# Expert stage of a decoder layer: gate2 multiplied into w2 on GpSimd instead of into the expert output on VectorE

## The chip, the cores and the metric

The kernel runs on one core of a Trainium2 chip, as one program for all five engines of the core: TensorE (PE in the profile; its weight loads are PEld), VectorE (DVE), ScalarE (ACT), GpSimd (POOL) and SyncE (SP, which here only starts transfers). The metric is the device time of one execution in microseconds (us).

## The reference, cut to what matters

```
h2  = modulate(rmsnorm(x, norm2_w), shift2, scale2)      # 4096 tokens x 1024
# each token goes to 2 of 32 experts, with one gate each:
hid = silu(xs @ w1[e]) * (xs @ w3[e])                    # 1024 -> 512
ys  = (hid @ w2[e]) * gate[token, e]                     # 512 -> 1024
ffn = segment_sum(ys over the two experts of a token)
x   = x + gate2 * ffn                                    # gate2: one row of 1024
out = rmsnorm(x, final_norm_w)
```

gate2 is one number for each of the 1024 columns, the same for every token and every expert. So gate2 * (hid @ w2) can be had by multiplying the columns of w2 instead of the columns of the product.

## The kernel before, in words

Stages A, B and C (projections, retention, delta rule, output projection, routing) come first and the change leaves them as they are. Stage D, the experts, is the subject: `phase_d` (L1150) and what it calls.

**Order of the experts.** The experts are sorted by how many tokens they have. Each rank has a fixed number of slots (`CAPS`: 832, 512, 512, 480, 480, 448, 384, 352, three times 320, three times 288, eleven times 240, seven times 128). They are taken alternately from both ends of that list: the largest, the smallest, the second largest, and so on. An expert is cut into chunks of at most three tiles of up to 128 rows (a tile is what the second layer adds at a time). So there are 16 pairs: seven of a large expert and one of 128 slots, seven of an expert with three tiles (352 to 288) and one of 240 (two tiles), and two of 240 and 240.

**Weights.** `load_expert` (L1327) brings an expert in 12 blocks of 128 x 1024 numbers: eight for w1 and w3, then four for w2. For each block SP starts a transfer into one of five `rawD` buffers (L1333), ScalarE makes the rounded half `whD` (L71, in the helper `split`), and VectorE makes the rest `wlD` = rawD - whD (L72). Both halves go to slots of a pool of 27, of which one expert takes 24 and the three gather buffers `xg` the others, so a block of the next expert can only be split when TensorE has used up a block of the present one. The first eight blocks of the next expert are asked for while the last chunk of the present one runs, the four of w2 at the start of the expert's own first chunk (`load(r, 12)`, L1228).

**One chunk.** `d_hidden` (first layer): for each of four column groups 24 matmuls into `ph` for w1 and 24 for w3, Silu on ScalarE, the product `hs` on VectorE (L1448), then `hh` and `hl`, its two halves. Chunks of 128 slots go another way with rows and columns exchanged (L1471 to L1479). `d_rows` (second layer): for each tile two halves of 512 columns, each 12 matmuls into one of two `py` buffers (L1535 to L1537). Then `add` (L1539): VectorE takes `py` times the token's gate times gate2 into `yg` (L1542), and adds `yg` to `ag` (L1543), the 128 rows of the running sum. Between the tiles TensorE transposes the next chunk's rows (`ptx`, L1413), which ScalarE and VectorE split into `xh` and `xl`.

**The running sum** lies in device memory (`acc_d`). Its rows are gathered by GpSimd into one of four `ag` buffers (`d_acc`, L1490), and scattered back when the tile is added (`keep`, L1570). Columns beyond 1024 hold a flag from which `d_to` (L1503 to L1506) computes where to write. In the next chunk VectorE scales the finished rows in place (L1380) and GpSimd scatters them to the output (L1381). All GpSimd work of the stage is one queue: gathers of `xg` (L1397) and of `ag`, the flags, `keep`, the output.

**What sets the order.** The instructions of each engine are put in a fixed order by a scheduler when the program is built; `pin` (L1350) ties a GpSimd instruction behind the one that the program wrote before it on GpSimd. On the chip each engine takes its instructions in that order.

Of the kernel before, what the change touches and what calls it, by code (L numbers as in the profile page):

```python
# [9 lines left out]
F32 = mybir.dt.float32  # L10
# [4 lines left out]
ALU = mybir.AluOpType  # L15
# [4 lines left out]
P = 128  # L20
D = 1024
# [32 lines left out]
class Kern:  # L54
# [1097 lines left out]
    def phase_d(self):  # L1152
        tc, nc, T = self.tc, self.nc, self.T
        caps = [min(c, T) for c in self.CAPS]
        with tc.tile_pool(name="D", bufs=2) as p:
# [15 lines left out]
            n = 0  # L1171
            for r in order:
                col0[r] = n
                rows = [min(P, caps[r] - P * b) for b in range(nt[r])]
                i = 0
# [13 lines left out]
            def load_slots(i):  # L1189

                r = order[i]
                c = slice(col0[r], col0[r] + nt[r])
                reg[r] = nc.values_load(self.eid[0:1, r:r + 1], engines=[mybir.EngineType.SP], min_val=0, max_val=NE - 1)
                nc.sync.dma_start(slots[:, c], tab[bass.ds(reg[r], 1), :, 0:nt[r]].rearrange("o l b c -> (o l) b c"))
                nc.vector.tensor_copy(ids[:, c], slots[:, c, 0])
# [3 lines left out]
            def load(r, k):  # L1199

                if r not in ld:
                    ex[r] = {"w1": {}, "w3": {}, "w2": {}}
                    ld[r] = self.load_expert(p, reg[r], ex[r])
                for _ in range(k):
                    next(ld[r], None)
# [15 lines left out]
            for i, s in enumerate(st):  # L1221
                nx = st[i + 1] if i + 1 < len(st) else None
                r = s["r"]
                if s["first"]:
                    k = order.index(r)
                    if k + 2 < len(order):
                        load_slots(k + 2)
                    load(r, 12)  # L1228
                if i == 2:
                    li, limb, col = self.overflow(p, caps)  # L1230
                if nx:
                    self.d_gather(p, nx, ids)

                jobs = []
                if s["last"] and nx:
                    jobs += [lambda: load(nx["r"], 2)] * 4

                pv = st[i - 1] if i else None
                acc = [lambda t=t, m=m: self.d_acc(p, s, t, m, ids) for t, m in s["tiles"]]
                free = self.AGS - (len(pv["tiles"]) if pv else 0)  # L1240
                ends = [acc[:free], acc[free:] + [lambda: self.d_to(p, s, slots)]]
                if pv:
                    ends[0].insert(0, lambda: self.d_norm(p, pv))
                    ends[1].insert(0, lambda: self.d_root(p, pv))
                    ends[1][1:1] = [lambda q=q: self.d_out(p, pv, q) for q in range(len(pv["tiles"]))]
                self.d_hidden(p, s, ex[r], jobs[:2], ends)
                turn = self.d_turn(p, nx) if nx else []
                self.d_rows(p, s, ex[r], slots, turn, jobs[2:], nx is None)
            self.outs = None
            n = nc.values_load(li[0:1, 2 * P:], min_val=0, max_val=P - 1)  # L1250
            with tc.For_i(0, n, 1) as i:
# [10 lines left out]
                s = dict(tiles=[(0, P)], n=P, rows=False)  # L1262
# [64 lines left out]
    def load_expert(self, p, e, w):  # L1327


        nc = self.nc  # L1330

        def block(raw, src, dst, key, n):
            nc.sync.dma_start(raw.rearrange("p (k n) -> p k n", n=n), src)  # L1333
            hi, lo = self.wtile("whD"), self.wtile("wlD")
            self.split(hi[:, 0:1024], lo[:, 0:1024], raw)
            dst[key] = [t[:, 0:1024].rearrange("p (k n) -> p k n", n=n) for t in (hi, lo)]

        for a in range(2):
            for nm, src in (("w1", self.w1), ("w3", self.w3)):
                s = src[0, bass.ds(e, 1)].rearrange("o (k p) n -> p (o k) n", p=P)  # L1340
                for q in range(2):
                    raw = p.tile([P, 1024], F32, name="rawD", bufs=self.RAWS)
                    block(raw, s[:, 4 * q:4 * q + 4, 256 * a:256 * a + 256], w[nm], (a, q), 256)
                    yield
        s = self.w2[0, bass.ds(e, 1)].rearrange("o (k p) n -> p (o k) n", p=P)
        for k in range(4):
            raw = p.tile([P, 1024], F32, name="rawD", bufs=self.RAWS)
            block(raw, s[:, k:k + 1], w["w2"], k, 1024)
            yield
# [158 lines left out]
    def d_rows(self, p, s, w, slots, turn, jobs, last):  # L1508

        nc, T = self.nc, self.T  # L1510
        turn, jobs = list(turn), list(jobs)
        hh, hl = s["hh"], s["hl"]
        NH = 2 * len(s["tiles"])

        def turns(k):
            for _ in range(k):
                if turn:
                    turn.pop(0)()

        turns(2)  # L1520
        per = -(-len(turn) // max(1, NH - 1))
        o = 0
        for q, (t, m) in enumerate(s["tiles"]):
            agw = s["ag"][t]
            ag = agw[:, 0:D]
            gate = slots[0:m, t, 1:2]
            to = s["to"][t]
            py = [self.psum([P, 512], "py", "ch")[0:m] for _ in range(2)]

            def part(i, ks):  # L1530
                cs = slice(512 * i, 512 * i + 512)
                for k in ks:
                    hi, lo = (b[:, 0, cs] for b in w["w2"][k])
                    a, b = hh[k][:, o:o + m], hl[k][:, o:o + m]
                    nc.tensor.matmul(py[i], a, hi, start=(k == 0), stop=False)  # L1535
                    nc.tensor.matmul(py[i], a, lo, start=False, stop=False)  # L1536
                    nc.tensor.matmul(py[i], b, hi, start=False, stop=(k == 3))  # L1537

            def add(i):  # L1539
                cs = slice(512 * i, 512 * i + 512)  # L1540
                yg = p.tile([P, 512], F32, name="yg", bufs=3)[0:m]
                nc.vector.scalar_tensor_tensor(yg, py[i], gate, self.g2[0:m, cs], op0=ALU.mult, op1=ALU.mult)  # L1542
                nc.vector.tensor_tensor(ag[0:m, cs], ag[0:m, cs], yg, op=ALU.add)  # L1543

            if q == 0:

                first = range(2) if s["late"] else range(3)
                for i in range(2):
                    part(i, first)
                if s["late"]:  # L1550
                    s["late"]()
                    turns(2)
                for i in range(2):
                    part(i, range(len(first), 4))
                    add(i)
                    turns(per)
                if jobs:
                    jobs.pop(0)()
            else:
                for i in range(2):  # L1560
                    part(i, range(4))
                    add(i)
                    turns(per)
            if jobs and q == len(s["tiles"]) - 1:
                for f in jobs:
                    f()
                jobs = []

            def keep(agw=agw, to=to, m=m):
                self.pin(nc.gpsimd.indirect_dma_start(out=self.acc_d,  # L1570
                                                      out_offset=bass.IndirectOffsetOnAxis(ap=to[0:m, 0:1], axis=0),
                                                      in_=agw[0:m], in_offset=None, bounds_check=T - 1,
                                                      oob_is_err=False))

            keep()
            o += m
        turns(len(turn))
        if last:
            self.d_norm(p, s)
            self.d_root(p, s)  # L1580
            for q in range(len(s["tiles"])):
                self.d_out(p, s, q)
# [37 lines left out]
```

## Time and profile before

| | |
|---|---|
| time, median of 3 runs | 4055.59 us (4050.54 to 4057.15) |
| the profiled execution's own time | 4068.07 us |
| its span, from the first to the last instruction | 4066.3 us |
| of that, stages A to C | about 2600 us |
| first matmuls of stage D to last additions | 2640 to 4040 us |
| VectorE busy in the whole span | 2550.0 us (63%) |
| GpSimd busy in the whole span | 1565.0 us (38%) |

A profile is of one execution: every duration and every wait below is from that one, whose time is 12.5 us above the median of the runs. "Busy" counts time with an instruction on the engine; for TensorE a matmul that waits for its turn behind another is busy too. A wait is idle time of an engine, with what ended it behind the arrow "<-". All times in the rows count from the span's start. Where a time is given in a bracket at the end of a row, it is the idle time of the engine before that instruction.

### The profile page before, as it was taken

How to read it: one execution, taken by the hardware profiler on the slowest of the kernel's cores; microseconds unless marked ns; L12 is line 12 of the kernel's file. 1: busy time of each engine (PE TensorE's matmuls, PEld its weight loads, DVE VectorE, ACT ScalarE, POOL GpSimd, SP SyncE). 2: the span in 40 equal slices, each digit the busy share in tenths (PEclk: the TensorE clock that was granted, in tenths of full speed). 3: DMA queues.
4: the chain of work that ended last, by engine and by line, in shares of the span. 5: the costliest groups of instructions: out<-in, count | busy, mean ns of one | idle time of the engine just before them, and what ended most of it. 6: DMA issues, size and time to landing. Idle time of an engine off the chain costs nothing.

```text
span 4066.3 us, 72672 instructions
## 1 busy us (share of the span) xinstructions
PE 3853.1 (95%) x26602; PEld 3477.2 (86%) x26602; DVE 2550.0 (63%) x6629; ACT 1602.7 (39%) x3309; POOL 1565.0 (38%) x2195
## 2 busy tenths in 40 slices
PE   5999999999999999979999999599999999999997
PEld 4888888899999999967888888498888889888887
DVE  6655544477777777753444444657777777767786
ACT  3433343444544444432222222224444444444453
POOL 2333333234433443413444444423333443444443
PEclk9999999999999999989999999799999999999999
DMA  6444323422122122356555554446666676666673
GB/s 197 133 135 123 101 76 107 117 60 74 45 68 74 49 67 72 95 160 197 166 169 178 180 170 142 157 134 213 220 215 215 217 238 197 228 202 212 227 241 131
DMA packets 483393, 609.99 MB, mean 150 GB/s; under 512 B 101088, under 2 KB 381384, under 8 KB 483032
## 3 DMA queue, kind: packets, MB, share of 16 engines
q1 hardware_dynamic: 429400, 480.98, 38.4%
q0 software_dynamic: 50592, 118.90, 8.6%
q10 hardware_dynamic: 3040, 5.43, 0.5%
q8 instruction: 211, 3.46, 0.3%
q14 instruction: 150, 1.23, 0.1%
HBM read 475.20 MB, written 183.03 MB: 162 GB/s over the span
## 4 chain that ended last, share of the span: by engine, by line
PE 75%; DMA 9%; DVE 8%; issue 3%; ACT 3%; POOL 1%; SPq 1%; POOLq 0%; DVEq 0%; ACTq 0%
PE ph L1443 5%; PE ph L1444 5%; PE ph L1442 5%; PE pjB L533 4%; PE pjB L534 4%; PE pjB L535 4%; PE py L1535 3%; PE py L1536 3%; PE py L1537 3%; PE poC L298 3%; PE poC L299 3%; PE poC L297 3%; PE pgz L297 3%; PE pgz L299 3%; PE pgz L298 3%
## 5 line engine op out<-in xcount | busy, mean ns | idle before, releaser
L1442 PE MATMUL ph<-xh,whD 128*128 128x240 f32 (+7 forms) x2048 | 580.6, 289 | 14.5 <-DVE ssD L1363 6.5
L1443 PE MATMUL ph<-xl,whD 128*128 128x240 f32 (+7 forms) x2048 | 588.4, 288 | 1.3 <-DVE xl L72 0.8
L1444 PE MATMUL ph<-xh,wlD 128*128 128x240 f32 (+7 forms) x2048 | 586.6, 288 | 0.0
L71 ACT ACTIVATE whD<-rawD 128x1024 fp32r<-128x1024 f32 x384 | 401.3, 1056 | 309.9 <-PE py L1536 127.0
L72 DVE TENSOR_TENSOR wlD<-rawD,whD 128x1024 fp32r<-128x1024 f32 x384 | 460.8, 1218 | 31.2 <-ACT whD L71 30.0
L533 PE MATMUL pjB<-hhB,whi 128*128 128x260 f32 x1536 | 446.2, 293 | 9.9 <-DVE cv L541 5.1
L534 PE MATMUL pjB<-hlB,whi 128*128 128x260 f32 x1536 | 442.8, 289 | 2.6 <-DMA hlB<-hl_d 2.5
L535 PE MATMUL pjB<-hhB,wlo 128*128 128x260 f32 x1536 | 443.5, 289 | 0.0
L1442 PEld LDWEIGHTS ph<-xh,whD 128*128 128x128 f32 x2048 | 388.5, 191 | 20.3 <-ACT xh L71 8.4
L1443 PEld LDWEIGHTS ph<-xl,whD 128*128 128x128 f32 x2048 | 391.1, 191 | 5.9 <-DVE xl L72 3.6
L1444 PEld LDWEIGHTS ph<-xh,wlD 128*128 128x128 f32 x2048 | 391.0, 191 | 1.9
L533 PEld LDWEIGHTS pjB<-hhB,whi 128*128 128x128 f32 x1536 | 292.0, 191 | 14.1 <-ACT beta L410 5.3
L534 PEld LDWEIGHTS pjB<-hlB,whi 128*128 128x128 f32 x1536 | 292.8, 191 | 6.4 <-DMA hlB<-hl_d 3.9
L543 POOL TENSOR_TENSOR cv<-cv,cv 128x256 f32<-128x256 f32 x192 | 141.9, 740 | 405.5 <-DVE Xd L613 142.1
L535 PEld LDWEIGHTS pjB<-hhB,wlo 128*128 128x128 f32 x1536 | 292.8, 191 | 1.6
L1535 PE MATMUL py<-whD,hh 128*128 128x512 f32 (+4 forms) x640 | 258.6, 404 | 12.3 <-ACT hh L71 6.5
L1536 PE MATMUL py<-wlD,hh 128*128 128x512 f32 (+4 forms) x640 | 251.9, 394 | 0.0
L1537 PE MATMUL py<-whD,hl 128*128 128x512 f32 (+4 forms) x640 | 246.0, 400 | 2.9 <-DVE hl L72 2.6
L1570 POOL DMA_INDIRECT acc_d<-ag,to x80 | 111.9, 1399 | 343.1 <-DVE ag L1543 245.7
L541 DVE SCALAR_TENSOR_TENSOR cv<-pjB,cw,cv 128x256 f32<-128x256 f32 x384 | 183.1, 479 | 85.6 <-ACT cv L539 78.5
L299 PE MATMUL pgz<-whi,hlC 128*128 128x512 f32 x512 | 203.8, 398 | 9.7 <-DMA hlC<-hl_d 9.7
L297 PE MATMUL pj<-whi,hh 128*128 128x512 f32 x512 | 205.5, 401 | 6.3 <-ACT whi L71 6.3
(459 smaller groups left out, 10125.9 us busy)
## 6 DMA issues: line engine op xcount, KB each, us to landing
rawD<-in_w_dram SPq DMA_DIRECT2D x384, 512.0 KB, 5.5
wa<-in_w_ada_dram SPq DMA_DIRECT2D x48, 512.0 KB, 4.8
hhB<-hh_d SPq DMA_DIRECT2D x64, 260.0 KB, 4.0
hlB<-hl_d SPq DMA_DIRECT2D x64, 260.0 KB, 4.6
acc_d<-xC SPq DMA_DIRECT2D x32, 520.0 KB, 2.6
wraw<-in_w_in_dram SPq DMA_DIRECT2D x32, 512.0 KB, 6.5
hh_d<-hh SPq DMA_DIRECT2D x16, 1024.0 KB, 7.5
hl_d<-hl SPq DMA_DIRECT2D x16, 1024.0 KB, 10.1
```

Of the source, the lines that this page charges most:

```text
L71: nc.scalar.activation(hi, src, AF.Copy)
L72: (e_lo or nc.vector).tensor_tensor(lo, src, hi.bitcast(F32) if hasattr(hi, "bitcast") else hi, op=ALU.subtract)
L297: nc.tensor.matmul(out, a, hi, start=(k == 0), stop=False)
L299: nc.tensor.matmul(out, b, hi, start=False, stop=(k == KD - 1))
L533: nc.tensor.matmul(pj, wh, hh[k], start=(k == 0), stop=False)
L534: nc.tensor.matmul(pj, wh, hl[k], start=False, stop=False)
L535: nc.tensor.matmul(pj, wl, hh[k], start=False, stop=(k == KD - 1))
L1442: nc.tensor.matmul(ph[nm], hi, xh[:, k, 0:n], start=(k == 0), stop=False)
L1443: nc.tensor.matmul(ph[nm], hi, xl[:, k, 0:n], start=False, stop=False)
L1444: nc.tensor.matmul(ph[nm], lo, xh[:, k, 0:n], start=False, stop=(k == KD - 1))
L1535: nc.tensor.matmul(py[i], a, hi, start=(k == 0), stop=False)
L1536: nc.tensor.matmul(py[i], a, lo, start=False, stop=False)
```

## The change

It has three parts. In `load_expert`, when a block of w2 has landed (n is 1024 for those alone), GpSimd multiplies it in place by the row of gate2, which lies in 128 copies in `g2`; the multiplication is pinned to its place in GpSimd's queue, and ScalarE's and VectorE's split of the block come behind it. In `add`, the two VectorE instructions become one: `ag` = `py` times gate plus `ag`. And in `phase_d`, `load(r, 12)` stands behind `d_gather` instead of ahead of it.

```
                 if k + 2 < len(order):
                     load_slots(k + 2)
-                load(r, 12)
             if i == 2:
                 li, limb, col = self.overflow(p, caps)
             if nx:
                 self.d_gather(p, nx, ids)
+            if s["first"]:
+                load(r, 12)
...
         def block(raw, src, dst, key, n):
             nc.sync.dma_start(raw.rearrange("p (k n) -> p k n", n=n), src)
+            if n == D:
+
+                self.pin(nc.gpsimd.tensor_tensor(raw, raw, self.g2, op=ALU.mult))
             hi, lo = self.wtile("whD"), self.wtile("wlD")
             self.split(hi[:, 0:1024], lo[:, 0:1024], raw)
...
             def add(i):
                 cs = slice(512 * i, 512 * i + 512)
-                yg = p.tile([P, 512], F32, name="yg", bufs=3)[0:m]
-                nc.vector.scalar_tensor_tensor(yg, py[i], gate, self.g2[0:m, cs], op0=ALU.mult, op1=ALU.mult)
-                nc.vector.tensor_tensor(ag[0:m, cs], ag[0:m, cs], yg, op=ALU.add)
+                nc.vector.scalar_tensor_tensor(ag[0:m, cs], py[i], gate, ag[0:m, cs], op0=ALU.mult, op1=ALU.add)
```

Behind the first place the lines of the changed kernel have other numbers: L1401 is the gather of `xg`, L1494 that of `ag`, L1572 `keep`, L1385 the output, L1337 the new multiplication, L1545 the one instruction of `add`.

GpSimd's queue between an expert of three tiles and the one of 240 behind it, in the late pairs, before:

```order
L1397 DMA xg<-h_d,ids 128x1024
L1397 DMA xg<-h_d,ids 32x1024
L1570 DMA acc_d<-ag,to 4096x1040 x3
L1490 DMA ag<-acc_d,ids 128x1040
L1381 DMA out_dram<-ag,to 4096x1024 x2
```

And the same place now:

```order
L1401 DMA xg<-h_d,ids 128x1024
L1401 DMA xg<-h_d,ids 32x1024
L1337 TENSOR_TENSOR rawD<-rawD,g_28189 128x1024 x4
L1572 DMA acc_d<-ag,to 4096x1040 x3
L1494 DMA ag<-acc_d,ids 128x1040
L1385 DMA out_dram<-ag,to 4096x1024 x3
```

All four multiplications of the 240 expert's w2 stand ahead of the three `keep` of the expert in front of it.

GpSimd's queue from the second half of a large expert into the expert of 128 slots and the next large one, before:

```order
L1397 DMA xg<-h_d,ids 128x1024
L1570 DMA acc_d<-ag,to 4096x1040 x2
L1490 DMA ag<-acc_d,ids 128x1040
L1397 DMA xg<-h_d,ids 128x1024 x2
L1381 DMA out_dram<-ag,to 4096x1024 x2
```

And now:

```order
L1337 TENSOR_TENSOR rawD<-rawD,g_28189 128x1024
L1401 DMA xg<-h_d,ids 128x1024
L1337 TENSOR_TENSOR rawD<-rawD,g_28189 128x1024 x3
L1572 DMA acc_d<-ag,to 4096x1040 x2
L1494 DMA ag<-acc_d,ids 128x1040
L1401 DMA xg<-h_d,ids 128x1024
L1337 TENSOR_TENSOR rawD<-rawD,g_28189 128x1024
L1401 DMA xg<-h_d,ids 128x1024
L1337 TENSOR_TENSOR rawD<-rawD,g_28189 128x1024 x3
L1385 DMA out_dram<-ag,to 4096x1024 x2
```

Four multiplications (of the small expert's w2) stand ahead of `keep`, and four more (of the next large one's) between the small expert's gather of `ag` and the output of the rows in front.

VectorE's queue in the rows of an expert of three tiles (288 slots), before:

```order
L1542 SCALAR_TENSOR_TENSOR yg<-py,slots,g_28189 128x512 x2
L72 TENSOR_TENSOR xl<-ptx,xh 128x4x112
L1543 TENSOR_TENSOR ag<-ag,yg 128x512 x2
L1542 SCALAR_TENSOR_TENSOR yg<-py,slots,g_28189 128x512
L1543 TENSOR_TENSOR ag<-ag,yg 128x512
L1542 SCALAR_TENSOR_TENSOR yg<-py,slots,g_28189 128x512
L1543 TENSOR_TENSOR ag<-ag,yg 128x512
L1542 SCALAR_TENSOR_TENSOR yg<-py,slots,g_28189 32x512
L1543 TENSOR_TENSOR ag<-ag,yg 32x512
L72 TENSOR_TENSOR wlD<-rawD,whD 128x1024
```

And now:

```order
L1545 SCALAR_TENSOR_TENSOR ag<-py,slots,ag 128x512 x2
L72 TENSOR_TENSOR xl<-ptx,xh 128x4x112
L1545 SCALAR_TENSOR_TENSOR ag<-py,slots,ag 128x512 x2
L1545 SCALAR_TENSOR_TENSOR ag<-py,slots,ag 32x512
L72 TENSOR_TENSOR wlD<-rawD,whD 128x1024
L1545 SCALAR_TENSOR_TENSOR ag<-py,slots,ag 32x512
```

Each half tile has one instruction instead of two; the splits of the weights stand between them as before.

## Rows read from the trace of the kernel before

**Rows 1.** The page: its first line.

```profile
span 4066.3 us, 72672 instructions
```

**Rows 2.** Windows, stage D: length, then busy time and instructions of each engine, clock, DMA.

```profile
2640.00:4040.00 1400.00, 1358.59 (x9272) 1238.55 (x9270) 1010.30 (x1812) 624.48 (x934) 563.65 (x621) 0.99 0.64 210
```

**Rows 3.** Waits of PE in stage D: us in total, times, longest.

```profile
PE ptx L1413 <- DVE xl L72: 10.3, 12, 1.5
PE ph L1442 <- DVE ssD L1363: 6.5, 3, 3.6
PE py L1535 <- ACT hh L71: 6.5, 5, 2.4
...
PE plst L1320 <- DVE xl L72: 0.3, 1, 0.3
```

**Rows 4.** Groups of instructions of DVE, stage D: count | busy us, mean ns | idle before.

```profile
L72 DVE TENSOR_TENSOR wlD<-rawD,whD 128x1024 fp32r<-128x1024 f32 x374 | 448.7, 1218 | 22.9 <-ACT whD L71 21.7
L1542 DVE SCALAR_TENSOR_TENSOR yg<-py,slots,g 128x512 f32<-128x512 f32 (+4 forms) x160 | 116.4, 747 | 133.6 <-PE py L1537 133.1
L1543 DVE TENSOR_TENSOR ag<-ag,yg 128x512 f32<-128x512 f32 (+4 forms) x160 | 107.6, 686 | 7.5 <-DMA ag<-acc_d,ids 3.8
L1380 DVE SCALAR_TENSOR_TENSOR ag<-ag,ssD,fw 128x1024 f32<-128x1024 f32 (+4 forms) x80 | 99.8, 1281 | 37.0 <-DMA acc_d<-ag,to 36.0
```

**Rows 5.** Groups by shape, POOL, whole span: the product's nearest row (stage C).

```profile
L994 POOL TENSOR_TENSOR h2C<-h2C,B 128x1024 f32<-128x1024 f32 x31 | 74.2, 2395 | 39.6 <-DVE h2C L993 21.2 <-PE poC L299 8.8 <-DVE ohg L1026 3.9
```

**Rows 6.** Timeline of all engines, 2171.7 to 2176: start us, us, engine, instruction.

```profile
2171.74 2.41 POOL L994 TENSOR_TENSOR h2C<-h2C,B 128x1024 f32<-128x1024 f32 x1 [1.47 <-PE poC L299]
2172.16 3.15 DVE L72 TENSOR_TENSOR ml<-tr,mh 128x512 fp32r<-128x512 f32 x2 [0.56 <-ACT mh L71]
```

**Rows 7.** All instructions that write `ml`: shortest/median/longest ns.

```profile
L72 DVE TENSOR_TENSOR ml<-tr,mh x62: 675/683/2544, 1818.5 to 2552.7; 128x512 fp32r<-128x512 f32 x62
```

**Rows 8.** Timeline of all engines, 3825 to 3834.

```profile
3828.15 4.66 POOL L1505 TENSOR_SCALAR to<-ag,slots 112x1 int32<-112x1 f32 x1
...
3828.67 1.22 DVE L72 TENSOR_TENSOR wlD<-rawD,whD 128x1024 fp32r<-128x1024 f32 x1
3829.80 0.68 DVE L1543 TENSOR_TENSOR ag<-ag,yg 112x512 f32<-112x512 f32 x1
3830.41 2.35 DVE L72 TENSOR_TENSOR wlD<-rawD,whD 128x1024 fp32r<-128x1024 f32 x2
```

**Rows 9.** The page's group of the split's first half, whole span.

```profile
L71 ACT ACTIVATE whD<-rawD 128x1024 fp32r<-128x1024 f32 x384 | 401.3, 1056 | 309.9 <-PE py L1536 127.0
```

**Rows 10.** Timeline of POOL, 3780 to 3800, a late pair.

```profile
3785.51 0.92 POOL L1397 DMA_INDIRECT xg<-h_d,ids  x1 [0.30 <-issue]
3786.74 1.32 POOL L1570 DMA_INDIRECT acc_d<-ag,to  x1 [0.30 <-DVE yg L1542]
...
3799.34 2.60 POOL L1570 DMA_INDIRECT acc_d<-ag,to  x1 [8.20 <-DVE ag L1543]
```

**Rows 11.** The line of `keep`, stage D: who waited for it; its transfers.

```profile
  POOL acc_d L1570: 26.4, 5
...
DMA to landing us min/median/max: 2.1/4.4/10.0
```

**Rows 12.** Timeline of DVE, 3808 to 3813, the same late pair.

```profile
3808.84 3.67 DVE L1380 SCALAR_TENSOR_TENSOR ag<-ag,ssD,fw 128x1024 f32<-128x1024 f32 x3
```

**Rows 13.** Timeline of all engines, 2947 to 2958, around a small expert.

```profile
2950.52 0.28 DVE L72 TENSOR_TENSOR hl<-pth,hh 128x128 fp32r<-128x128 f32 x1
...
2950.79 2.35 DVE L72 TENSOR_TENSOR wlD<-rawD,whD 128x1024 fp32r<-128x1024 f32 x2
...
2953.13 1.28 DVE L72 TENSOR_TENSOR xl<-ptx,xh 128x512 fp32r<-128x512 f32 x2
...
2953.84 0.99 PE L1442 MATMUL ph<-xh,whD 128*128 128x256 f32 x3
```

**Rows 14.** Timeline of all engines, 4030 to 4067, the last addition.

```profile
4046.85 0.69 DVE L1543 TENSOR_TENSOR ag<-ag,yg 112x512 f32<-112x512 f32 x1
```

More of the change, by code (lines that the diff above doesn't have):

```diff
@@ L1227, in phase_d @@
                         load_slots(k + 2)
-                    load(r, 12)
                 if i == 2:
@@ L1232, in phase_d @@
                     self.d_gather(p, nx, ids)
+                if s["first"]:
+                    load(r, 12)
                 jobs = []
@@ L1333, in block @@
             nc.sync.dma_start(raw.rearrange("p (k n) -> p k n", n=n), src)
+            if n == D:
+                self.pin(nc.gpsimd.tensor_tensor(raw, raw, self.g2, op=ALU.mult))
             hi, lo = self.wtile("whD"), self.wtile("wlD")
@@ L1540, in add @@
                 cs = slice(512 * i, 512 * i + 512)
-                yg = p.tile([P, 512], F32, name="yg", bufs=3)[0:m]
-                nc.vector.scalar_tensor_tensor(yg, py[i], gate, self.g2[0:m, cs], op0=ALU.mult, op1=ALU.mult)
-                nc.vector.tensor_tensor(ag[0:m, cs], ag[0:m, cs], yg, op=ALU.add)
+                nc.vector.scalar_tensor_tensor(ag[0:m, cs], py[i], gate, ag[0:m, cs], op0=ALU.mult, op1=ALU.add)
             if q == 0:
```

## The prediction

> **What bounds the kernel now.** I read the span first [rows 1], then the windows: in the 1400 us of stage D that the change touches TensorE is busy 1358.59 us, VectorE 1010.30, ScalarE 624.48 and GpSimd 563.65 [rows 2]. TensorE is the bound, so taking work off another engine is worth at most what TensorE waits for that engine. That I read from TensorE's waits: ten kinds that VectorE or ScalarE ends, 40.4 us together; the three largest are 10.3, 6.5 and 6.5 us [rows 3]. They come in bursts at the 16 pairs, where VectorE splits the weights of two experts (1218 ns a block) back to back [rows 4].
>
> **What the change removes.** 160 additions of 686 ns, 107.6 us of VectorE [rows 4]. The new instruction has `py` and one SBUF tensor as operands, as the one it replaces, so I take the latter's 747 ns [rows 4]. Most of the 107.6 us is covered already: VectorE stands idle 133.1 us in this stage ahead of L1542, waiting for the next `py` [rows 4], so an addition taken away there lengthens that idle time. What can come back is bounded by nothing at one end and the 40.4 us of TensorE's waits at the other [rows 3]. I take one addition for each burst, as a wait for `xl` is a wait for whatever stands just ahead of it: 16 x 0.69 = 11 us back. At the end of the kernel the last addition, 0.69 us, is on the path [rows 14]: 0.7 back.
>
> **What it adds.** 32 experts x 4 blocks = 128 products on GpSimd. No row of this stage shows one; stage C has the same shape, operands and engine at 2395 ns [rows 5]: 128 x 2.4 = 307 us. GpSimd is busy 563.65 of 1400 us [rows 2], so it has the room. Whether the product delays the split: ScalarE's longest wait ahead of that line is for TensorE to leave a slot of the pool at the end of the second layer, 127.0 us [rows 9]; the block has landed by then and the product fits in front. I cost that at nothing; if the product were late every time by its own length it would be the 307 us.
>
> **First price: VectorE shut out.** Beside L994 a VectorE subtraction with two SBUF inputs stays until GpSimd's instruction ends: two that usually take 683 ns each [rows 7] took 3.15 us together, and the first ended where the GpSimd one did (2171.74 + 2.41 = 2174.15) [rows 6]; the longest took 2544 ns [rows 7]. So a product holds up the next `wlD`, and all that stands behind it on VectorE. In a large expert's rows this lands in the idle 133.1 us. Around the seven small experts it does not: four products of the next large expert fall, by the order, around GpSimd's gathers there, and VectorE's row is full: `hl` at 2950.52 reads PSUM and lets GpSimd in, then two `wlD`, then `xl` at 2953.13, with which TensorE starts the next expert at 2953.84 [rows 13]. One product ahead of those two `wlD` moves `xl` and TensorE by 2.4 us. The bounds are nothing (VectorE catches up with the additions that it no longer makes) and 4 x 2.4 = 9.6 us; I take one product, as TensorE stands close behind VectorE at one place: 7 x 2.4 = 17 us.
>
> The trace has a second side to this: a GpSimd instruction on one column took 4.66 us while VectorE ran four instructions with two SBUF inputs back to back, and it ended with the last of them [rows 8]. [...] If runs of four products do that to VectorE too, one batch costs 9.6 us; that is the last rival below.
>
> **Second price: `keep` behind the products.** In the seven pairs of a three-tile expert and one of 240, the four products stand between the last gather of `xg` and the first `keep`. Now that gather ends at 3785.51 + 0.92 and the first `keep` starts at 3786.74, the third at 3799.34 [rows 10]. With four products: 3786.43 + 0.3 + 9.6 = 3796.3 for the first. A `keep` waits for the landing of the one in front (five such waits, 26.4 us; median 4.4 us to land [rows 11]), so the second starts at about 3796.3 + 1.0 + 4.4 = 3801.7, the third at 3807.1, and that one lands at 3812.5. Who waits: VectorE scales those rows in place and has to wait for the landing (36.0 us of such waits now [rows 4]); behind it stand the splits and the `xl` that TensorE waits for. The third scaling starts now at 3808.84 + 2/3 x 3.67 = 3811.3 [rows 12]. So at least 1.2 us late; and where each product first waits for a `wlD` of 1.22 us to end, 4 x 1.22 = 4.9 more: 6.1. I take the middle, 3.6: 7 x 3.6 = 25 us. The bounds are 0 (the scheduler has put other work ahead of the scaling) and 43.
>
> **Moved code.** `load(r, 12)` behind the gather: SP's transfers keep their order, and GpSimd's gather goes ahead of the products. Nothing.
>
> **Sum**, on the profiled execution: 4068.07 - 11 - 0.7 + 17 + 25 = 4098, that is 30 us more. That execution lies 12.5 us above the median of the runs, 4055.59; so I forecast 4086 us, and for this case by itself 4064 to 4110. A change of 0.2%, 8.1 us, is about the least that a measurement of this kernel can tell.
>
> **The rivals.** *Faster: the products are hidden and VectorE's relief counts.* For it: GpSimd idles 1400 - 563.65 = 836 us of the stage [rows 2], and 307 us of products fit into that; the new instruction has one SBUF operand only. Against it: TensorE waits for VectorE and ScalarE just 40.4 us in all [rows 3]. Half of that and the end: 4055.6 - 20 - 0.7 = 4035. Chance 0.22.
>
> *No difference: both effects cancel or both are hidden,* since TensorE has 97% of the stage [rows 2]. What speaks against it is that the two places with a price lie just where TensorE stands close behind VectorE. 4048 to 4064; chance 0.20.
>
> *Much slower: a batch keeps VectorE out as a whole.* Then VectorE's work in stage D is 1010.3 - 107.6 + 307 = 1210 of 1400 us, and in each of the 16 bursts, which are full now, a batch of four lengthens it by 9.6 us: 16 x 9.6 - 12 = 142 us, 4198 us. It decides from the point where VectorE gets nothing in between two products. For it stands the 4.66 us row, against it that the products of a batch wait for four transfers one after another, and that the splits of the same blocks wait for them too, so the batch is seldom dense. Chance 0.10.
>
> **Chances.** My forecast's own case 0.48, much slower 0.10: slower 0.58; within 0.2% 0.20; faster 0.22. For 8 times in 10 the range leaves out about a tenth at each side: the lower half of the faster case (4038) and the much slower case above 4150.
>
> **What would show it.** Right: in the trace after, L1337 128 times at about 2.4 us; single `wlD` of 2 to 3.6 us; the waits of TensorE in stage D for VectorE and ScalarE up from 40 to about 70 us, at the small experts behind `xl`, in the late pairs behind the scaling; the first `keep` of a three-tile expert some 10 us behind its gather. Wrong: `wlD` no longer than now, or long ones only where VectorE had idle time, and TensorE's waits at 40 us or below; then VectorE's relief was worth what it looked like. Wrong the other way: ScalarE waiting for L1337 ahead of `whD`, which I cost at nothing.

## The result, and the profile after

| | before | after |
|---|---|---|
| time, median | 4056.37 us (4 runs) | 4156.04 us (4 runs, 4143.73 to 4159.96) |
| ratio | | 1.0237 (95%: 1.0219 to 1.0255) |
| the profiled execution's own time | 4068.07 us | 4159.96 us |

The kernel is 2.4% slower, 100 us. I had forecast 30 us slower and a range up to 4150 us: the sign was right, the size was not, and the time lies 6 us outside the range.

First the page's first line of the kernel after, and its group of the added instruction (count | busy us, mean ns | idle before):

```profile
span 4158.2 us, 72742 instructions
...
L1337 POOL TENSOR_TENSOR rawD<-rawD,g 128x1024 f32<-128x1024 f32 x128 | 308.2, 2430 | 29.7 <-DVE hl L72 9.4
```

128 products of 2430 ns: number and duration are what I had taken from stage C [rows 5]. They are hidden on GpSimd itself. The windows of the kernel after, with the columns of [rows 2], show stage D and three stretches in it that are used below:

```profile
2640.00:4130.00 1490.00, 1390.44 (x9262) 1262.34 (x9261) 1075.42 (x1658) 628.35 (x935) 851.90 (x747) 0.96 0.60 197
3140.00:3156.00 16.00, 13.94 (x106) 12.96 (x104) 10.88 (x9) 6.21 (x9) 9.54 (x10) 1.00 0.71 249
3156.00:3167.00 11.00, 5.87 (x23) 5.29 (x24) 7.99 (x7) 0.93 (x1) 4.16 (x3) 0.53 0.18 52
3167.00:3200.00 33.00, 26.63 (x165) 22.52 (x164) 29.07 (x38) 19.41 (x27) 15.97 (x9) 0.95 0.72 239
```

The stage is some 90 us longer for the same work. VectorE is busy 65 us more although 108 us of additions are gone, and TensorE's mean clock fell from 0.99 to 0.96. TensorE's waits in stage D (2640 to 4160 us) are the counterpart of [rows 3]:

```profile
PE py L1539 <- DVE hh L69: 32.2, 10, 7.2
PE py L1541 <- DVE hl L72: 17.9, 7, 3.7
PE ph L1447 <- DVE xl L72: 12.0, 6, 4.6
PE ph L1446 <- DVE hs L1452: 11.3, 7, 4.9
PE py L1539 <- ACT hh L71: 11.0, 10, 2.3
PE ptx L1417 <- DVE xl L72: 9.2, 7, 5.3
PE ph L1446 <- ACT xh L71: 4.1, 5, 2.5
```

With one row of 0.8 us that is left out here they come to 98.5 us; in the kernel before all of them come to 40.4. The largest are no longer `xl` but `hh` and `hl`, which VectorE makes just ahead of the second layer, with single waits of up to 7.2 us. VectorE's groups, against [rows 4]:

```profile
L72 DVE TENSOR_TENSOR wlD<-rawD,whD 128x1024 fp32r<-128x1024 f32 x376 | 512.6, 1376 | 61.3 <-ACT whD L71 58.9 <-PE ph L1476 1.0
L1545 DVE SCALAR_TENSOR_TENSOR ag<-py,slots,ag 128x512 f32<-128x512 f32 (+4 forms) x160 | 116.1, 746 | 181.3 <-PE py L1541 167.6 <-PE py L1540 7.4 <-DMA ag<-acc_d,ids 6.2
L1384 DVE SCALAR_TENSOR_TENSOR ag<-ag,ssD,fw 128x1024 f32<-128x1024 f32 (+4 forms) x80 | 99.8, 1281 | 23.4 <-DMA acc_d<-ag,to 22.5
L442 DVE TENSOR_TENSOR rb_t<-rb_y 128x2 f32<-128x2 f32 (+2 forms) x117 | 39.2, 335 | 2.7
```

The new add takes what the old gating step took (746 and 747 ns). `wlD` went from 1218 to 1376 ns in the mean, and an instruction on two columns (L442; its median is 0.16 us) has a mean of 335. The means hide a few very long ones. One of them, in the timeline of all engines of the kernel after:

```profile
3146.13 5.72 DVE L72 TENSOR_TENSOR wlD<-rawD,whD 128x1024 fp32r<-128x1024 f32 x3
...
3147.46 3.31 POOL L1337 TENSOR_TENSOR rawD<-rawD,g 128x1024 f32<-128x1024 f32 x1 [5.74 <-DVE wlD L72]
...
3149.15 0.39 PE L1540 MATMUL py<-wlD,hh 128*128 128x512 f32 x1
...
3150.93 1.90 POOL L1401 DMA_INDIRECT xg<-h_d,ids  x1 [0.16 <-DMA rawD<-in_w_dram]
...
3152.08 8.82 DVE L72 TENSOR_TENSOR wlD<-rawD,whD 128x1024 fp32r<-128x1024 f32 x1
...
3152.85 6.95 POOL L1337 TENSOR_TENSOR rawD<-rawD,g 128x1024 f32<-128x1024 f32 x3
...
3153.66 0.28 PE L1476 MATMUL ph<-wlD,xh 128*128 128x256 f32 x1
3160.82 0.26 DVE L69 CAST hh<-hs 128x224 fp32r<-128x224 f32 x1
...
3161.13 0.79 PE L1539 MATMUL py<-whD,hh 128*128 128x512 f32 x1 [7.19 <-DVE hh L69]
...
3161.72 0.63 PE L1540 MATMUL py<-wlD,hh 128*128 128x512 f32 x1
```

Read it from the gather at 3150.93. When GpSimd has issued it, three blocks of w2 are ready, and it runs three products without a pause. VectorE's `wlD` started 0.77 us ahead of them, yet it takes 8.82 us and ends 1.1 us behind the last product: 7.6 us were lost in one place, not one product's 2.4. Behind it in VectorE's row stands `hh`; TensorE has nothing to do until `hh` is there, 7.19 us. In the window from 3156 to 3167 its granted clock is 0.53 (0.50 from 3158 to 3166), after 16 us at 1.00: the `py` matmul at 3161.72 takes 0.63 us, the same line at 3149.15 took 0.39. This wait is paid for once as idle time and once in slow matmuls.

To size the two, take for every two neighbouring matmuls of the stage the time from start to start above what the same neighbours take in the median of the kernel before. Where the second one waited, that adds up to 37 us before and 96 after; where none waited but the granted clock was 0.50, to 12 and 43. So of the 92 us by which the profiled span grew, about 60 are waits and about 30 are slow matmuls at that clock. It was the granted one for 27 us of stage D before and for 106 us after, mostly in stretches of 3 to 10 us.

On VectorE 54 instructions of stage D take over 0.3 us more than the median of their shape, 158 us together; in the kernel before there is none. 23 of them are stretched by more than one product's 2.4 us, 8 by more than 5 us. Between two products that follow each other there are 67 boundaries in this trace. At 31 of them a VectorE instruction was being held; it got in at 5 and was kept out at 26.

### The profile page after: what moved, and what is told of

Same layout as the page of the kernel before. It is cut to its first block, busy times and chain, and to the rows that moved or that the text cites. A ratio compares the mean times of both kernels' runs of the same rounds, so it can differ in the third digit from the quotient of the medians.

```text
span 4158.2 us, 72742 instructions
## 1 busy us (share of the span) xinstructions
PE 3888.8 (94%) x26602; PEld 3506.0 (84%) x26602; DVE 2612.9 (63%) x6469; ACT 1604.5 (39%) x3309; POOL 1855.7 (45%) x2323
## 4 chain that ended last, share of the span: by engine, by line
PE 68%; DVE 12%; DMA 10%; issue 4%; ACT 3%; POOL 3%; SPq 1%; POOLq 0%; DVEq 0%; ACTq 0%
PE ph L1447 4%; PE ph L1446 4%; PE ph L1448 4%; PE pjB L534 3%; PE pjB L533 3%; PE pjB L535 3%; DVE wlD L72 3%; PE poC L298 3%; PE poC L299 3%; PE poC L297 3%; PE pgz L297 3%; PE pgz L299 3%; PE pgz L298 3%; PE pj L297 3%; PE pj L298 3%
## 5 line engine op out<-in xcount | busy, mean ns | idle before, releaser
L72 DVE TENSOR_TENSOR wlD<-rawD,whD 128x1024 fp32r<-128x1024 f32 x384 | 522.3, 1373 | 68.7 <-ACT whD L71 66.4
L1447 PEld LDWEIGHTS ph<-xl,whD 128*128 128x128 f32 x2048 | 394.0, 192 | 17.8 <-DVE xl L72 15.3
L1337 POOL TENSOR_TENSOR rawD<-rawD,g 128x1024 f32<-128x1024 f32 x128 | 308.2, 2430 | 29.7 <-DVE hl L72 9.4
L1541 PE MATMUL py<-whD,hl 128*128 128x512 f32 (+4 forms) x640 | 254.2, 411 | 18.6 <-DVE hl L72 17.9
L1545 DVE SCALAR_TENSOR_TENSOR ag<-py,slots,ag 128x512 f32<-128x512 f32 (+4 forms) x160 | 116.1, 746 | 181.3 <-PE py L1541 167.6
```

The costliest lines, as they stand in the source:

```text
L72: (e_lo or nc.vector).tensor_tensor(lo, src, hi.bitcast(F32) if hasattr(hi, "bitcast") else hi, op=ALU.subtract)
L1337: self.pin(nc.gpsimd.tensor_tensor(raw, raw, self.g2, op=ALU.mult))
L1447: nc.tensor.matmul(ph[nm], hi, xl[:, k, 0:n], start=False, stop=False)
```

## The experiments

Each time is the median of several runs; the difference is to the median of the kernel before on the same chip (4060.65, 4062.01 and 4057.20 us for the three groups of four runs).

| run | what it is | us | difference | ratio (95%) |
|---|---|---|---|---|
| after | the change | 4156.0 | +100 | 1.0237 (1.0219 to 1.0255) |
| e1_no_product | no product | 4049.5 | -11 | 0.9975 (0.9961 to 0.9988) |
| e2_product_only | product, old add | 4210.6 | +150 | 1.0377 (1.0345 to 1.0409) |
| e3_free_split | split doesn't wait, products spaced | 4112.1 | +51 | 1.0137 (1.0105 to 1.0170) |
| e4_on_vector | product on VectorE | 4111.4 | +51 | 1.0131 (1.0099 to 1.0162) |
| e5_gap | products spaced | 4134.0 | +72 | 1.0187 (1.0161 to 1.0212) |
| e6_free_run | split doesn't wait, not spaced | 4137.4 | +75 | 1.0196 (1.0170 to 1.0223) |
| e7_quarters | four short products each | 4152.0 | +90 | 1.0221 (1.0195 to 1.0247) |
| e8_one_input | one tensor input | 4072.0 | +10 | 1.0029 (1.0014 to 1.0045) |
| e9_late_only | last 18 experts only | 4072.8 | +16 | 1.0050 (1.0033 to 1.0067) |
| e10_small_only | first 14 experts only | 4120.8 | +64 | 1.0157 (1.0140 to 1.0174) |
| e11_early_load | load at its old place | 4279.0 | +222 | 1.0555 (1.0537 to 1.0572) |
| e12_free_one_input | one input, split doesn't wait | 4073.0 | +16 | 1.0049 (1.0028 to 1.0070) |

Theory 1: GpSimd's products keep VectorE out of SBUF for a whole run of them. Rival 2: what costs is that the splits of w2 wait for the product's data (in the trace after, ScalarE's `whD` waits 99.6 us for line 1337).

**e1_no_product.** The relief alone.

```diff
-            if n == D:
-                self.pin(nc.gpsimd.tensor_tensor(raw, raw, self.g2, op=ALU.mult))
```

> The kernel after without the 128 products on GpSimd; the fused add and the later load stay, and gate2 is left out of the result. What the removed adds are worth by themselves. My sum gave 11 us for them, so 4045 us beside 4056 of before. Theory 1 (GpSimd's products keep VectorE out of SBUF for a whole batch): 4035 to 4050, and no stretched VectorE instruction is left. Rival (the fused add itself, or the load that stands later, costs something): over 4056.

11 us faster than before, and `wlD` is nowhere longer than 1268 ns:

```profile
L72 DVE TENSOR_TENSOR wlD<-rawD,whD x384: 1201/1220/1268, 2607.7 to 3998.7; 128x1024 fp32r<-128x1024 f32 x192
```

(The view groups a tile's instructions: shortest/median/longest ns.) The 11 us of my sum were right: 108 us of VectorE's work are worth a tenth of that. The product therefore costs 111 us.

**e2_product_only.** The price alone, with the old two-step add (the diff is the change without its last hunk).

> The kernel before with the 128 products and the later load, and its own two-step add kept, so that gate2 is applied twice. The price without the relief. If relief and price simply add, it is 4156 + 11 = 4167 us. Theory 1: 4160 to 4190, since VectorE has 107 us more to do and each time it is kept out costs at least as much. If VectorE's adds had been worth more in the kernel after than in the kernel before (less slack there), it is over 4190.

150 us slower than before, above the range that I had given for theory 1: the third case of what I expected. With the products there, the removed adds are worth 50 us, not 11: the old add has two inputs in SBUF and is itself shut out. In that trace it is L1547, with single instructions of up to 10.2 us and 110 of the 237 us by which VectorE's instructions are stretched:

```profile
L1547 DVE TENSOR_TENSOR ag<-ag,yg 128x512 f32<-128x512 f32 (+4 forms) x160 | 225.5, 1423 | 4.9 <-DMA ag<-acc_d,ids 3.0
```

Its mean is 1423 ns, in [rows 4] 686. Relief and price do not add up as two terms, as my sum had them.

**e3_free_split.** The product reads the block but writes elsewhere, so the split doesn't wait for it.

```diff
-                self.pin(nc.gpsimd.tensor_tensor(raw, raw, self.g2, op=ALU.mult))
+                self.pin(nc.gpsimd.tensor_tensor(self.g2, raw, self.fw, op=ALU.mult))
```

> The product still reads each block of w2 as it arrives, at the same place in GpSimd's order, but multiplies it by the final norm's weight and writes into gate2's tile, so that the split of the block waits for the transfer alone (gate2 is left out of the result). Theory 1 (shared access to SBUF): the products still keep VectorE out in batches; 4120 to 4160 us, with VectorE instructions of 4 to 9 us beside runs of products. Rival 2 (what costs is that the splits of w2 wait for the product's data, the 99.6 us that ScalarE waits for line 1337): back to 4040 to 4065.

+51 us, between the two: 49 us less than after, 62 more than without a product. The longest `wlD` is 4232 ns, in the kernel after it was 8816:

```profile
L72 DVE TENSOR_TENSOR wlD<-rawD,whD x384: 1201/1218/4232, 2607.3 to 4055.7; 128x1024 fp32r<-128x1024 f32 x192
```

This run had changed two things. Every product now writes the same tile, so each waits for the one ahead: in the trace about 80 ns lie between products that stand next to each other in 36 of 41 cases, more in the others, while in the kernel after the next product starts 30 to 70 ns before the one ahead ends (67 times). (The ends of GpSimd's instructions are rough in this profile; from start to start it is 2.36 us there and 2.49 us here, in the median.) A VectorE instruction was being held at 17 of the 36 boundaries with a gap of 80 ns, and got in at all 17. Hence e5 and e6, which change one of the two each.

**e5_gap.** The split waits as in the kernel after, but the products are spaced.

```diff
                 self.pin(nc.gpsimd.tensor_tensor(raw, raw, self.g2, op=ALU.mult))
+                self.pin(nc.gpsimd.tensor_scalar(self.one, raw[:, 1023:1024], 1.0, None, op0=ALU.mult))
```

> The kernel after with a one-column GpSimd instruction behind each product that reads the product's last column, so that the next product cannot start before this one is finished. In the kernel after the next product starts 30 to 70 ns before the one ahead ends; where each had to wait for the one ahead (the run with the free split) 80 ns lay between them, and no VectorE instruction took longer than 4.23 us beside 8.82 and 9.95 us. Theory 1 (VectorE gets SBUF back only in a gap between GpSimd instructions): longest stretched VectorE instruction under 4.5 us, and 4110 to 4140 us. Rival 2 (the split's wait for the product is what the run with the free split took away, the gap does nothing): 4145 to 4170 us.

+72 us, and the longest VectorE instruction of the stage takes 4.26 us: theory 1, by 28 us. (Here 0.25 us or more lie between the products, as the one-column instruction stands there.) The place of the timeline above, in this kernel:

```profile
3130.91 1.88 POOL L1403 DMA_INDIRECT xg<-h_d,ids  x1 [0.16 <-DMA rawD<-in_w_dram]
...
3132.02 4.25 DVE L72 TENSOR_TENSOR wlD<-rawD,whD 128x1024 fp32r<-128x1024 f32 x1
...
3132.82 2.36 POOL L1338 TENSOR_TENSOR rawD<-rawD,g 128x1024 f32<-128x1024 f32 x1
3135.27 1.08 POOL L1339 TENSOR_SCALAR one<-rawD 128x1 f32<-128x1 f32 x1
3136.20 0.29 DVE L69 CAST hh<-hs 128x224 fp32r<-128x224 f32 x1
3136.32 2.38 POOL L1338 TENSOR_TENSOR rawD<-rawD,g 128x1024 f32<-128x1024 f32 x1
...
3136.54 0.50 PE L1541 MATMUL py<-whD,hh 128*128 128x512 f32 x1 [2.91 <-DVE hh L69]
```

Same `wlD`, same gather, same three products (two are shown): VectorE gets its turn behind the first product, `hh` follows, and TensorE waits 2.91 us instead of 7.19. The other 72 us remain. VectorE's instructions are still stretched by 134 us in all, 158 in the kernel after, now by one product at a time, and the split still waits for its block.

**e6_free_run.** As e3, but the products write to two places in turn and so overlap again.

```diff
+                self.n_h = getattr(self, "n_h", 0) + 1
+                h = self.g2.bitcast(BF)[:, 1024 * (self.n_h % 2):1024 * (self.n_h % 2) + 1024]
-                self.pin(nc.gpsimd.tensor_tensor(raw, raw, self.g2, op=ALU.mult))
+                self.pin(nc.gpsimd.tensor_tensor(h, raw, self.fw, op=ALU.mult))
```

> As the run with the free split (the product reads each block but the split doesn't wait for it, gate2 left out), but the products write to two places in turn, in bf16, so that they can follow each other without a gap. Theory 1: VectorE instructions of 6 to 10 us are back, and 4125 to 4160 us. Rival 2 (all that the free split gained, it gained from the splits that don't wait): 4100 to 4120 us, like the 4112 us of that run.

+75 us, and VectorE instructions of up to 7.2 us from 2640 us on (9.9 us at 2629): theory 1 again. e6 minus e3 is 24 us, after minus e5 28 us: the missing gap costs about 25 us whether the split waits or not. After minus e6 is 24 us, e5 minus e3 21 us: the split's wait costs a little over 20 us whether there is a gap or not. The two effects add to each other, but not to the whole: with both taken away, e3 is still 62 us above the kernel without products. (A part of the 24 us may be shorter runs: 4 of 68 hold four products in e6, 12 of 61 in the kernel after.)

The 9.9 us instruction at 2629 is the longest `wlD`:

```profile
L72 DVE TENSOR_TENSOR wlD<-rawD,whD x384: 1201/1218/9890, 2607.6 to 4076.4; 128x1024 fp32r<-128x1024 f32 x192
```

**e7_quarters.** Each product in four.

```diff
-                self.pin(nc.gpsimd.tensor_tensor(raw, raw, self.g2, op=ALU.mult))
+                for c in range(0, 1024, 256):
+                    self.pin(nc.gpsimd.tensor_tensor(raw[:, c:c + 256], raw[:, c:c + 256], self.g2[:, c:c + 256], op=ALU.mult))
```

> Each product cut into four of 256 columns, one behind the other, nothing else changed. If VectorE is let in at every end of a GpSimd instruction (the reading of my prediction, one instruction at a time), no VectorE instruction is stretched by more than some 0.7 us, and the time is 4090 to 4120 us. If it is let in only where a gap lies between two (theory 1 now), the quarters of a batch that overlap keep it out as before: 4150 to 4175 us and stretches of 6 to 10 us.

+90 us, and the longest VectorE instruction takes 7.82 us (`hl`, three times, each beside twelve quarters without a gap). If VectorE were let in at each end of a GpSimd instruction it could not wait longer than a quarter. But it did get in more often: about one quarter-product in six was itself held up,

```profile
L1338 POOL TENSOR_TENSOR rawD<-rawD,g 128x256 f32<-128x256 f32 x502 | 440.0, 911 | 25.0 <-DVE hl L72 13.1 <-DMA rawD<-in_w_dram 5.3 <-DVE hs L1453 5.0
```

so that their mean is 911 ns where most take 0.7 us, and 10 us were won. Where VectorE was being held, it got in at about half of the boundaries between quarters, between whole products at 5 of 31. What decides who wins at a boundary without a gap is not settled by these runs.

**e8_one_input and e12_free_one_input.** A GpSimd instruction with one tensor input at the same place; in e12 it writes elsewhere, so that the split doesn't wait.

```diff
-                self.pin(nc.gpsimd.tensor_tensor(raw, raw, self.g2, op=ALU.mult))
+                self.pin(nc.gpsimd.tensor_scalar(raw, raw, 1.0, None, op0=ALU.mult))      # e8
+                self.pin(nc.gpsimd.tensor_scalar(h, raw, 1.0, None, op0=ALU.mult))        # e12, h as in e6
```

> A GpSimd instruction with one tensor input (the block times 1.0, in place) at the place of the product; gate2 is left out. The split still waits for GpSimd. If the wait for the data alone is what costs, and one input doesn't take SBUF from VectorE: 4070 to 4110 us and no stretched VectorE instruction. If GpSimd takes it with one input as well: 4130 to 4160 us, with stretches as in the kernel after.

> The GpSimd instruction with one tensor input again, but written to gate2's tile (two places in turn), so that the split doesn't wait for it; gate2 is left out. With the split waiting it was 22 us above the kernel without any product (4072 beside 4049). If that was the wait for the data: 4045 to 4058 us. If it was the access to SBUF also with one input: 4062 to 4080 us.

+10 and +16 us. e8's rows, the added instruction and the longest `wlD`:

```profile
L1337 POOL TENSOR_SCALAR rawD<-rawD 128x1024 f32<-128x1024 f32 x124 | 352.9, 2864 | 27.1 <-DVE hl L72 9.2 <-issue 7.2 <-DVE wlD L72 4.2
...
L72 DVE TENSOR_TENSOR wlD<-rawD,whD x384: 1201/1219/2899, 2606.6 to 4032.7; 128x1024 fp32r<-128x1024 f32 x192
```

This instruction is longer than the product (2864 against 2430 ns), stands at the same place, is waited for by the same splits and overlaps where one follows the other as well (124 x 2864 ns are 355.1 us, in which GpSimd is busy 352.9; for the product 128 x 2430 ns are 311.0 us, busy 308.2). Yet it costs 90 us less, no VectorE instruction takes over 2.9 us, and all that are stretched come to 66 us, not 158. So most of the price is neither GpSimd's time nor what stands behind the product in GpSimd's queue; it goes with the two-input product. The operation changed along with the number of inputs (`tensor_scalar` for `tensor_tensor`), so that the second input by itself is the cause is likely but not shown. e12 is not faster than e8: with one input the wait for the data costs nothing that can be measured. Of the two expectations for e12 the time by access holds, but the 20 us above e1 can be access to SBUF or a later GpSimd queue; no run separates these two.

**e4_on_vector.** The product on VectorE.

```diff
-                self.pin(nc.gpsimd.tensor_tensor(raw, raw, self.g2, op=ALU.mult))
+                nc.vector.tensor_tensor(raw, raw, self.g2, op=ALU.mult)
```

> The same product on VectorE instead of GpSimd, everything else as after. By the nearest row (the two-input wlD of 128x1024, 1.31 us), 128 x 1.3 = 170 us are added to VectorE and 110 us of adds are gone. Theory 1: no second engine takes SBUF away, so 4050 to 4095 us, nearer to 4065, although VectorE has 60 us more work than in the kernel before. Rival 2 (w2's halves are simply ready one product later): still 4110 to 4160.

+51 us: 16 us above theory 1's range, at the lower end of rival 2's, and still 49 us better than on GpSimd, with 156 us more work on VectorE (128 x 1218 ns, not the 1.3 us that I had put down). What TensorE waits for speaks against rival 2: not w2's halves but `xl`, in many short waits, most of them ahead of `ptx`. No instruction is stretched there; VectorE is simply late. The product's row (124 of 128 in the window) and the largest wait:

```profile
L1337 DVE TENSOR_TENSOR rawD<-rawD,g 128x1024 f32<-128x1024 f32 x124 | 150.9, 1218 | 25.7 <-DMA rawD<-in_w_dram 25.4
...
PE ptx L1417 <- DVE xl L72: 35.0, 21, 4.2
```

**e9_late_only and e10_small_only.** Where the loss lies: the product and the fused add for one part of the experts, the old add without a product for the rest.

```diff
+                    ld[r] = self.load_expert(p, reg[r], ex[r], order.index(r) >= 14)      # e9;  < 14 in e10
...
-            if n == D:
+            if n == D and mul:
```

> Product and fused add only for the last 18 experts of the order (three tiles and 240 rows); the first 14, the pairs with the seven small experts, keep the two-step add and have no product. Where the loss lies. By my prediction the larger part (25 of 42 us) is here: 4056 + 25 - 6 = 4075 us or more, by waits of the scaling behind the keeps. By the trace of the kernel after, the second part of the stage grew from 612.8 to 628.3 us: 4072 us, without such waits. If the products were harmless away from the small experts: 4048 to 4056 us, faster than before.

> The other half: product and fused add only for the first 14 experts of the order, the pairs with the seven small experts. By the trace of the kernel after, this part grew by 92.6 - 15.5 = 77 us: 4133 us. By my prediction 17 us less some 5 for the removed adds: 4068 us.

+16 us for the 18 late experts, as the trace had it, and +64 for the first 14, less than the trace's 77 and nearly four times the prediction's 17; 80 together. The 20 missing to 100 appear only with both. The pairs with a small expert carry most of it, 64/7 = 9 us a pair, close to the 9.6 us that I had as the upper bound there. But they are not one batch of four at one place: 38 VectorE instructions are stretched there, five a pair, by 2.5 us in the mean; 8 of the 38 by more than one product. That the late experts' 16 us come near the prediction's 25 less 6 is luck, as the mechanism that I gave isn't there: VectorE's scaling waits less than before for `keep` to land (L1385 in e9, L1380 in [rows 4], 36.0 us there):

```profile
L1385 DVE SCALAR_TENSOR_TENSOR ag<-ag,ssD,fw 128x1024 f32<-128x1024 f32 (+4 forms) x80 | 99.8, 1281 | 12.7 <-DMA acc_d<-ag,to 11.6
```

**e11_early_load.** The load of the expert ahead of the gather again.

```diff
                         load_slots(k + 2)
+                    load(r, 12)
...
-                if s["first"]:
-                    load(r, 12)
```

> The kernel after with the load of the expert back at its old place, ahead of the gather of the next rows: the third part of the change undone. I cost the move at nothing. If it matters, then because GpSimd's gather stands behind four products now (10 us): 4160 to 4200 us, with TensorE's transposes waiting for the gathered rows. If the move does nothing: 4148 to 4164 us.

+222 us: the part of the change that looked like bookkeeping saves 122 us of the price. Neither of my two expectations held: the time is far above both, and TensorE doesn't wait for the gathered rows but for `wlD` and `hs`:

```profile
PE py L1539 <- DVE wlD L72: 72.5, 13, 9.7
PE ph L1445 <- DVE hs L1451: 43.9, 13, 5.5
PE ptx L1416 <- DVE xl L72: 16.9, 11, 3.1
```

The trace shows two reasons. The products come later: 24 of the 25 runs of four stand directly behind a `keep`, which waits for VectorE's last addition of a tile, so w2's halves are still missing when TensorE comes to the second layer. And they are dense: counting products with no more than 0.1 us between them, 25 runs hold four here, and 12 of 61 in the kernel after. How much each of the two costs I did not separate.

## Why the prediction was wrong

*VectorE bounded by TensorE's waits; 160 adds worth 11 us.* Right in e1, which measured 11 us. But it holds only without the products: e2 shows 50 us with them.

*128 products at 2.4 us, room on GpSimd.* Right: 2430 ns, and GpSimd is busy 852 of 1490 us.

*The split's wait for the product, costed at nothing.* Partly wrong. The trace shows the wait that I had named as the sign of it, ScalarE waiting for L1337:

```profile
ACT whD L71 <- POOL rawD L1337: 99.6, 40, 6.7
```

It costs a little over 20 us (after against e6, e5 against e3), and nothing with an instruction of one input (e8 against e12). This suggests that the wait matters only while the product keeps VectorE from the splits that it releases.

*First price, one product of 2.4 us at each of seven places, 17 us.* This is the step that failed. The mechanism was right, its size was not: the pairs with a small expert cost 64 us instead of 17 (e10). The count of places was the larger error. I had one held instruction for each pair; the trace of e10 has five, as it happened to instructions with all their inputs in SBUF, from `wlD` to a two-column `rb_t`, and in front of `hh` and `hl` rather than only of `xl`. The length was the other: where products followed each other without a gap, VectorE was shut out for the run, at worst 7 to 10 us, and not for one of them. With a gap behind each product (e5) that second error is gone, and 83 of the 111 us that the product costs are still there, some 20 of them by the split's wait. I had bounded a place at 9.6 us and chosen 2.4 because TensorE "stands close behind VectorE at one place"; the trace of the kernel after shows several places a pair, and a whole run falling at one of them.

*Second price, `keep` behind four products, 25 us.* It did not come as a wait for landings. The first `keep` is late as I said, 9.7 us behind the end of the gather, in the timeline of POOL of the kernel after, at the pair of the same sizes as in [rows 10]:

```profile
3857.48 0.93 POOL L1401 DMA_INDIRECT xg<-h_d,ids  x1 [1.95 <-PE ptx L1417]
3858.43 9.47 POOL L1337 TENSOR_TENSOR rawD<-rawD,g 128x1024 f32<-128x1024 f32 x4
3868.07 1.03 POOL L1572 DMA_INDIRECT acc_d<-ag,to  x1 [0.17 <-issue]
3871.73 0.98 POOL L1572 DMA_INDIRECT acc_d<-ag,to  x1 [2.63 <-DMA acc_d<-ag,to]
3876.25 3.79 POOL L1572 DMA_INDIRECT acc_d<-ag,to  x1 [3.54 <-DVE ag L1545]
```

The second waits for the landing of the first, as I had it. But the third waits for VectorE's addition of TensorE's last tile, as before. It starts 18.8 us behind the gather's start, in [rows 10] 13.8 and in my sum 21.6; and the gather itself now runs ahead of the expert's first addition, so that from that addition it is 18.6 us, and was 17.8. The scaling waited 22.5 us for landings, 36.0 before.

*Moved code: nothing.* Wrong in a way that the sum did not show: the kernel after contains the move, and e11 says that without it the price would be twice as high.

*A term that I did not have:* the slow matmuls while TensorE's granted clock was 0.50, about 30 of the 92 us by which the profiled span grew.

*The rivals.* The mechanism of the one called much slower, with a chance of 0.10, is a part of what happened: a run of products without a gap mostly keeps VectorE out as a whole, and the missing gap costs 28 us (after against e5). Its 142 us took every batch as dense; of 61 runs of products 12 were of four, 13 of three, 5 of two and 31 of one. I had the row for it, 4.66 us [rows 8], and set it aside because the batch "is seldom dense". The order of GpSimd's queue goes with it: 28 of the 30 runs of two or more stand directly behind a gather. That the blocks which land while it waits or is issued are then ready together is my reading, which no run tests by itself.

In these traces the end of a product was mostly not the end of VectorE's wait where the next one followed without a gap: kept out at 26 boundaries of 31, 8.82 us beside three products, for a `wlD` that by the trace had started 0.77 us ahead of them; 4.25 us at the same place with a gap. Beside GpSimd's one-input instruction (e8) no VectorE instruction took over 2.9 us. The new add, which reads `py` from PSUM, was never longer than 754 ns in the kernel after, although 44 of the 160 ran beside a product.

No version that I ran beats the kernel before while it applies gate2. e1 puts what the removed adds give in a kernel without products at 11 us, and the cheapest way that I measured of having GpSimd touch all the blocks of w2 costs 21.

## What to carry to other kernels

Work moved to an idle engine is not free where a busy engine's instructions get longer beside it: here 54 of VectorE's, by 158 us together, all with their inputs in SBUF. Before counting the moved work's length, count those, and what waits behind them. That count was the larger error here. Then look for runs: several such instructions ready at once can act as one of their total length, as three products did on a `wlD` of 8.82 us. Here a small gap between them gave back 28 us, a one-input instruction in the product's place 90, and instructions a quarter as long 10. And a wait of the bounding engine costs more than its length where its clock falls with it: about 30 of the 92 us here.

## What the runs showed of the hardware

- Products on GpSimd (two SBUF inputs) that follow each other directly overlap by 30 to 70 ns in the profile of the kernel after, and VectorE mostly did not get in between them (5 of 31 times); with 80 ns between them it did (17 of 17 times, e3). The longest VectorE instruction of the stage takes 9.95 us in the kernel after, 7.2 in e6 and 4.2 in e3.
- GpSimd's one-input instruction of the same shape took longer (2864 ns in e8, 2430 in the kernel after) and VectorE was held up far less beside it (2.9 us at most, 9.95 in the kernel after), although it overlaps in a row as well (2.2 us in all, 2.8 for the products).
- Shut out in the kernel after were VectorE's instructions whose inputs all lie in SBUF, a two-column one with a single tensor input among them (`ssD`, 9.95 us where its median is 0.16). Those that read PSUM were not: the add took 754 ns at most (44 of 160 beside a product), `xl` 694 (40 of 160), `hl` from `pth` 293 (6 of 28).
- In the kernel after TensorE's granted clock was 0.53 in the 11 us around the end of a wait of 7.19 us, after 1.00, and a `py` matmul took 0.63 us there, 0.39 before.
